# Two plain blocks in place of three in three channel mixers, with low parts of weights on GpSimd and a 32-byte shift of token-mixer tiles

## The chip, the cores and the metric

The kernel runs on one core of a Trainium2 chip. The metric is the device time of one execution in microseconds. The engines are TensorE (PE; PEld are its weight loads), VectorE (DVE), ScalarE (ACT), GpSimd (POOL) and SyncE (SP, which issues most DMAs). Each works through its own list of instructions in order and waits on semaphores for the others.

## The reference

A decoder trunk of two layers on 512 tokens of width 1024, in float32. Each layer has a channel mixer, a token mixer and another channel mixer:

```
for i in range(2):
    h = h + 0.5 * swiglu(rmsnorm(h, ffn_norm_a[i]), ffn_a_w_gate[i], ffn_a_w_up[i], ffn_a_w_down[i])
    m = rmsnorm(h, mix_norm[i])
    h = h + (mla_mixer, nsa_mixer)[i](m, ...)
    h = h + 0.5 * swiglu(rmsnorm(h, ffn_norm_b[i]), ffn_b_w_gate[i], ffn_b_w_up[i], ffn_b_w_down[i])
return rmsnorm(h, final_norm)

def swiglu(x, w_gate, w_up, w_down):
    return (silu(x @ w_gate) * (x @ w_up)) @ w_down      # 1024 -> 2816 -> 1024
```

## The kernel before

Everything stays in SBUF transposed: `h` is eight tiles h0 to h7 of 128 channels by 512 tokens. A float32 product is made of three matmuls in the faster float32r form: each operand is split into a high part, rounded by ScalarE's copy, and a low part, the rest; then high x high, high x low and low x high are summed in PSUM (`mm3`, and the same three in `plain1` and `product`).

A channel mixer (`ffn`, called four times with idx 0 to 3; "second mixer" is idx 1, "third" idx 2, "fourth" idx 3) runs over 22 hidden blocks f of 128. The first `PLAIN = 3` blocks are plain: `plain` takes a weight slab of 128x1024 for the gate and one for the up projection, and for each of the eight chunks of `h` and each half of the tokens issues three matmuls of 256 columns, 96 for the block. The other 19 blocks use a scheme of seven products of sums in place of eight (`wsums` makes the sums of weights, `product` issues 12 matmuls per product, 84 for the block: `px`, `pq` and `pg` are its PSUM tiles). For that scheme the input is needed as sums too. `combine(p)` makes them for p = 0 to 3 from `h[p]` and `h[p + 4]`: two scaled copies on ScalarE (`y`, L267), three VectorE subtractions (`u`, L271 to L273) and a split (`four`, L205 on ScalarE and L206 on VectorE). The combines are spread over the plain blocks; in idx 1 to 3 as (0), (1), (2, 3).

A plain slab is loaded by SyncE into `wr` (two buffers) and split into `w` (two buffers, `wtiles`): `split` inside `slab_ahead` does the high part on ScalarE (L176) and the low part on VectorE in one step of 1024 columns (L178). If `lo_pool` is set, GpSimd makes the low part in two steps of 512 columns (L182). This is used in the token mixers only. `wsums` splits its slabs and sums through `Kern.split` (L205 and L206), eight VectorE steps for a block's sums and low parts, five of 512 columns and three of 1024.

After a block's products come `gate` (L433 to L435: `tg` from the gate's PSUM and the row of norm factors, silu on ScalarE), `act` (L444 or L446, then a split into `ah` and `al`) and, from block 3 on, units of the down projection over the previous three blocks (`unit`: a slab `wdr` split into `wd`, 9 matmuls of 512 columns into `pd`, and an addition into `h`, L457).

The norm of the input is not applied ahead of the products but to their results. At the start of a channel mixer the sums of squares of the last chunks are still being made: `sumsq` squares on ScalarE (L285, into a scratch tile `sq` with one buffer) and adds on GpSimd (L289, `s2`). `late` squares the last two chunks and `norm_col` sums over partitions on TensorE (`pc`, L311) and finds the inverse root on VectorE in twelve tiny steps (`small`, L294 to L304). In idx 2 and 3 `late` stands between the gate and up halves of block 0, in idx 1 behind both. After block 1 `norm_bcast` spreads the factors (`pb`, L323, and `row`).

`plain` asks for its slabs in the order of use; for idx 2 the first slab is split at the end of the mixer ahead (`ahead`, tile `ra`). The order on each engine is set by a scheduler that interleaves the recorded instructions, and `issue_after` holds some of them back.

The token mixers keep the negated norm factors in a tile of four columns of their own: `colq` in `mla` (L892, read by the softmax at L869) and `ncol` in `nsa` (L976, read at L1197 and L1236). `vtc` is a scratch of 12 columns whose columns 0 to 3 `rsqrt_col` uses while it finds the factors and not after. Tiles of one pool lie one behind another in SBUF, at steps of 32 bytes, and pools opened later lie behind them; so the size of `colq` and `ncol` decides where later tiles of the token mixers begin.

Of the kernel before, what the change touches and what calls it, by code (L numbers as in the profile page):

```python
# [11 lines left out]
F32 = mybir.dt.float32  # L12
# [6 lines left out]
P = 128  # L19
# [4 lines left out]
NF = FF // P  # L24
# [21 lines left out]
LASTK = 4  # L46
HS = S // 2
KP = KC // 2
PLAIN = 3
PAD = 16  # L50
TILES = 24
XC = P + 2
NG = 3
# [8 lines left out]
class Kern:  # L62
# [278 lines left out]
    def wsums(self, idx, f):  # L341


        nc, fp, w_gu = self.nc, self.fp, self.a["w_gu"]
        if f == PLAIN:

            rg = fp.tile([P, 1024], F32, tag="fr", bufs=3, name="rg")
        else:
            rg = self.wp.tile([P, 1024], F32, tag="wr", bufs=2, name="wr")
        nc.sync.dma_start(rg, w_gu[idx, f, 0])  # L350
        ru = fp.tile([P, 1024], F32, tag="fr", bufs=3, name="ru")
        nc.sync.dma_start(ru, w_gu[idx, f, 1])
        s1 = fp.tile([P, S], F32, tag="s1", bufs=1, name="s1")
        g0, g1, u0, u1 = rg[:, :S], rg[:, S:], ru[:, :S], ru[:, S:]

        def split(src, pool, tag, bufs):
            n = src.shape[1]
            if pool is self.wp:
                hi, lo = self.wtiles("half")
            elif n == 1024:  # L360
                hi, lo = self.sum_tiles(n)
            else:
                hi = pool.tile([P, n], F32R, tag=tag[0], bufs=bufs, name="wh")
                lo = pool.tile([P, n + 2 * PAD], F32R, tag=tag[1], bufs=bufs, name="wl")[:, 2 * PAD :]
            with self.tc.issue_after(self.evicted.ins) if f == PLAIN + 1 else nullcontext():
                self.split(src, hi, lo)
            return [(hi[:, x : x + S].rearrange("p (k c) -> p k c", c=P), lo[:, x : x + S].rearrange("p (k c) -> p k c", c=P))
                    for x in range(0, n, S)]

        w = {}  # L370
        w[1], w[2] = split(rg, self.wp, None, 2)
        nc.vector.tensor_tensor(s1, u0, u1, op=ALU.add)
        nc.vector.tensor_tensor(u0, u0, g0, op=ALU.add)
        w[7], w[4] = split(ru, fp, ("fh", "fl"), 3)
        nc.vector.tensor_tensor(g0, g0, s1, op=ALU.add)
        nc.vector.tensor_tensor(g1, g1, g0, op=ALU.add)
        w[6], w[3] = split(rg, fp, ("fh", "fl"), 3)
        w[5], = split(s1, fp, ("sh", "sl"), 2)
        return w
# [44 lines left out]
    def ffn(self, idx, gain_next, ap, tp):  # L424
        nc, a = self.nc, self.a
        self.scr, self.fp = (tp, "sq", 1), tp
        ah, al, ht, row = {}, {}, [], None
        tg, tu, units = {}, {}, []

        def gate(f, g):  # L430
# [6 lines left out]
        def tu_tile():  # L437
            return self.xp.tile([P, S], F32, tag="w2", bufs=2, name="tu")

        def act(f):  # L440
            t = tu[f]
            if f < PLAIN:
                t = tu_tile()
                nc.vector.scalar_tensor_tensor(t, tu[f], -1.0, tg[f], op0=ALU.mult, op1=ALU.mult)  # L444
            else:
                nc.vector.tensor_tensor(t, t, tg[f], op=ALU.mult)  # L446
            ah[f] = ap.tile([P, S], F32R, tag="act", bufs=4 * NG, name="ah")
            al[f] = ap.tile([P, S], F32R, tag="act", bufs=4 * NG, name="al")
            self.split(t, ah[f], al[f])
# [34 lines left out]
            return self.norm_col(D, self.s2)  # L484


        gates = [self.bank("T", "pg") for _ in range(PLAIN)]
        for f, g in enumerate(gates):
            u = tu[f] = self.bank(("mm", "S")[f % 2], "pu")
            if idx == f == 0:  # L490
# [29 lines left out]
            elif f:  # L520
                gate(f, g)
                act(f)
            for p in (((0,), (1,), (2, 3)) if idx else ((0, 1), (2,), (3,)))[f]:
                self.combine(p)
        t = self.tiny
        for i, g in enumerate(gates[::-1]):
            nc.scalar.activation(t[:, i + 1 : i + 2], g[:, 0:1], AF.Identity, bias=t[:, i : i + 1])

        tail = PLAIN + (NF - 2 - PLAIN) // NG * NG
        for f in range(PLAIN, NF):  # L530
            if f % NG == 0 and f <= tail:
                units = [partial(unit, b0=f - NG, c=c) for c in range(KC)]
                left = NG if f < tail else NF - tail
            n = -(-len(units) // left)
# [24 lines left out]
        if gain_next == "fin":  # L559

            hs, out = [self.parts(self.four(F32)) for _ in range(4)], []
            for t in range(4):
                for b in range(2):
                    p = self.mm_bank("ph")
# [9 lines left out]
        for c in self.order:  # L574
            p = self.mm_bank("pd")
# [143 lines left out]
    def mla(self, gain_next):  # L719
        nc, tc, a = self.nc, self.tc, self.a  # L720
        with ExitStack() as cx:
            mp = cx.enter_context(tc.tile_pool(name="mla", bufs=1))
# [60 lines left out]
            p = self.proj(a["mla_w_in"][5], P, xh, xl, "pr")  # L783
# [49 lines left out]
            def query_slab(t):  # L833
                return self.slab_ahead(a["mla_w_q"][t], (3, P), "act")
# [3 lines left out]
            def rows_of(w):  # L838
                return self.proj(None, P, cqh, cql, "pq", w)
# [49 lines left out]
                self.w_o1(w, oh[:4], ol[:4], c2 + KP * e, e, False)  # L889

            pq = [rows_of(query_slab(t)()) for t in range(3)]
            colq = mp.tile([P, 4], F32, name="colq")  # L892
            nc.vector.tensor_scalar(colq, self.norm_col(QL, s2q), -MLA_SCALE, None, op0=ALU.mult)
            wv = self.slab_ahead(a["mla_w_v"][0], (2, S), raw=self.xp.tile([P, 2 * S], F32, tag="x", bufs=KC, name="vr"))
            wk = self.slab_ahead(a["mla_w_k"][0:2].rearrange("a p c -> p a c"), (2, 2, P))
# [72 lines left out]
    def nsa(self, gain_next):  # L968
        nc, tc, a = self.nc, self.tc, self.a
        with ExitStack() as cx:  # L970
            mp = cx.enter_context(tc.tile_pool(name="nsa", bufs=1))
# [1 line left out]
            rvalid = self.gains[:, 53:57]  # L973
            gat = mp.tile([P, 4, 3 * H], F32, name="gat")
            gcmp = mp.tile([P, 4, H], F32, name="gcmp")
            ncol = mp.tile([P, 4], F32, name="ncol")  # L976


            kc = mp.tile([P, 96 + 2 * G * P + 32], F32R, name="kc")
# [543 lines left out]
```

## Time and profile before

| | us |
|---|---|
| runs of the kernel, median (lowest to highest) | 1866.38 (1865.87 to 1868.28) |
| the profiled execution, its own time | 1868.31 |
| its span, first to last instruction | 1866.5 |
| second, third and fourth mixer's first matmul | 548.97, 886.40, 1518.82 |
| their first product block's first matmul | 583.37, 920.47, 1553.22 |
| their next block's first matmul, after the units | 599.37, 936.52, 1569.48 |

The mean granted TensorE clock is 0.999 of full speed. In the rows of the trace a matmul's own duration (278 ns for 256 columns, 391 ns for 512) is longer than the step from one to the next, since matmuls overlap; the steps from start to start are what add up.

### The profile page before, as it was taken

The page shows a single profiled execution, that of the slowest core. Times are in us where ns is not written, and L with a number is a line of the kernel's source. Part 1 is how long each engine was busy: PE and PEld are TensorE (multiplying, and loading weights), DVE is VectorE, ACT ScalarE, POOL GpSimd, SP SyncE. Part 2 cuts the span into 40 slices and gives each one's busy share as a digit, 9 for nine tenths or more (in the row PEclk, how much of TensorE's full clock was granted, in tenths as well). Part 3 has the DMA queues.
Part 4 walks back from the last instruction along what each step waited for, and adds up shares of the span by engine and source line. Part 5 has one row for each costly group of instructions (what it writes and reads, how often), then busy time and mean ns, then how long its engine had stood idle before and what let it go on. Part 6 is the DMA issues. An engine that isn't in the chain of part 4 may idle for free.

```text
span 1866.5 us, 32992 instructions
## 1 busy us (share of the span) xinstructions
PE 1851.3 (99%) x12448; PEld 1687.5 (90%) x12448; DVE 1506.4 (81%) x2810; ACT 1068.2 (57%) x1997; POOL 296.4 (16%) x370
## 2 busy tenths in 40 slices
PE   9999999999999999999999999999999999999998
PEld 8999999888889999998999999988888889999997
DVE  8988886688779888886898888666877888888885
ACT  7555553567666555554655455445776865555554
POOL 0000000258830000001000000022666620000000
PEclk9999999999999999999999999999999999999999
DMA  6333331334433333322433332162433133333321
GB/s 236 126 114 102 102 91 47 116 101 106 114 122 112 118 102 102 107 77 67 136 124 111 106 106 84 44 175 86 110 108 102 37 119 122 114 105 106 102 77 70
DMA packets 84336, 196.38 MB, mean 105 GB/s; under 512 B 10945, under 2 KB 38465, under 8 KB 84177
## 3 DMA queue, kind: packets, MB, share of 16 engines
q1 hardware_dynamic: 81664, 191.34, 33.6%
q10 hardware_dynamic: 2512, 2.93, 0.5%
q8 instruction: 98, 1.61, 0.4%
q14 instruction: 62, 0.50, 0.1%
HBM read 178.44 MB, written 2.16 MB: 97 GB/s over the span
## 4 chain that ended last, share of the span: by engine, by line
PE 89%; DVE 4%; ACT 1%; issue 1%; POOL 1%; DMA 1%; SPq 0%; ACTq 0%; DVEq 0%; POOLq 0%
PE pd L198 8%; PE pd L197 8%; PE pd L199 8%; PE px L388 5%; PE px L386 5%; PE px L387 5%; PE pg L386 4%; PE pg L388 4%; PE pg L387 4%; PE pq L388 3%; PE pq L387 3%; PE pq L386 3%; PE o L1326 2%; PE pt L1299 2%; PE po L197 1%; PE po L199 1%
## 5 line engine op out<-in xcount | busy, mean ns | idle before, releaser
L198 PE MATMUL pd<-al,wd 128*128 128x512 f32 x576 | 225.3, 391 | 0.0
L197 PE MATMUL pd<-ah,wd 128*128 128x512 f32 x576 | 225.1, 391 | 0.0
L199 PE MATMUL pd<-ah,wd 128*128 128x512 f32 x576 | 224.9, 390 | 0.0
L289 POOL TENSOR_TENSOR s<-s,sq 128x512 f32<-128x512 f32 x38 | 54.8, 1441 | 1052.8 <-ACT sq L285 1052.7
L206 DVE TENSOR_TENSOR w<-wr,w 128x1024 fp32r<-128x1024 f32 x72 | 88.2, 1225 | 134.8 <-ACT w L205 134.5
L386 PE MATMUL px<-four,wh 128*128 128x256 f32 x608 | 168.7, 278 | 0.4 <-ACT pg L543 0.3
L388 PE MATMUL px<-four,wl 128*128 128x256 f32 x608 | 168.4, 277 | 0.2 <-DVE wl L206 0.2
L386 PE MATMUL pq<-four,wh 128*128 128x256 f32 x608 | 168.2, 277 | 0.0
L387 PE MATMUL px<-four,wh 128*128 128x256 f32 x608 | 168.2, 277 | 0.0
L388 PE MATMUL pq<-four,wl 128*128 128x256 f32 x608 | 168.1, 277 | 0.0
L387 PE MATMUL pq<-four,wh 128*128 128x256 f32 x608 | 168.1, 276 | 0.0
L457 DVE SCALAR_TENSOR_TENSOR h<-pd,h 128x512 f32<-128x512 f32 x216 | 148.6, 688 | 13.6 <-PE pd L199 13.6
L205 ACT ACTIVATE wd<-wdr 128x384 fp32r<-128x384 f32 x192 | 99.2, 519 | 95.8 <-ACT wd L205 58.1
L176 ACT ACTIVATE w<-wr 128x1024 fp32r<-128x1024 f32 (+3 forms) x89 | 80.8, 908 | 84.1 <-PE pd L199 19.2
L199 PEld LDWEIGHTS pd<-ah,wd 128*128 128x128 f32 x576 | 108.3, 188 | 22.7
L197 PEld LDWEIGHTS pd<-ah,wd 128*128 128x128 f32 x576 | 108.2, 188 | 20.4
L198 PEld LDWEIGHTS pd<-al,wd 128*128 128x128 f32 x576 | 108.2, 188 | 19.3
L178 DVE TENSOR_TENSOR w<-wr,w 128x1024 fp32r<-128x1024 f32 (+3 forms) x75 | 78.4, 1046 | 49.4 <-ACT w L176 49.0
L717 ACT ACTIVATE p<-p,small 128x512 f32<-128x512 f32 (+2 forms) x192 | 106.9, 558 | 19.3 <-DVE small L716 15.4
L386 PEld LDWEIGHTS px<-four,wh 128*128 128x128 f32 x608 | 114.2, 188 | 1.7 <-ACT pg L543 0.8
L388 PEld LDWEIGHTS px<-four,wl 128*128 128x128 f32 x608 | 114.2, 188 | 0.8 <-DVE wl L206 0.6
L386 PEld LDWEIGHTS pq<-four,wh 128*128 128x128 f32 x608 | 114.2, 188 | 0.4 <-ACT uq L545 0.4
(379 smaller groups left out, 6163.5 us busy)
## 6 DMA issues: line engine op xcount, KB each, us to landing
wr<-in_w_gu SPq DMA_DIRECT2D x93, 512.0 KB, 3.3
ru<-in_w_gu SPq DMA_DIRECT2D x76, 512.0 KB, 4.1
wdr<-in_w_down SPq DMA_DIRECT2D x192, 192.0 KB, 2.4
wr<-in_w_down SPq DMA_DIRECT2D x24, 256.0 KB, 2.7
wr<-in_mla_w_o SPq DMA_DIRECT2D x8, 512.0 KB, 3.8
th<-btab_d SPq DMA_DIRECT2D x16, 256.0 KB, 3.7
wr<-in_nsa_w_q SPq DMA_DIRECT2D x8, 512.0 KB, 3.9
wr<-in_nsa_w_o SPq DMA_DIRECT2D x8, 512.0 KB, 3.8
```

The source lines that it names most:

```text
L176: self.copied = nc.scalar.activation(wh[:, m], raw[:, m], AF.Copy)
L178: nc.vector.tensor_tensor(wl[:, m], raw[:, m], f32v(wh[:, m]), op=ALU.subtract)
L197: mm(out, wh, xh, start=first, stop=False)
L198: mm(out, wh, xl, start=False, stop=False)
L199: return mm(out, wl, xh, start=False, stop=last)
L205: nc.scalar.activation(hi, src, AF.Copy)
L206: (nc.gpsimd if pool else nc.vector).tensor_tensor(lo, src, f32v(hi), op=ALU.subtract)
L386: mm(out, wh[:, p], xh, start=first and p == 0, stop=False, skip_group_check=True)
L387: mm(out, wh[:, p], xl, start=False, stop=False, skip_group_check=True)
L388: mm(out, wl[:, p], xh, start=False, stop=last and p == KP - 1, skip_group_check=True)
L457: nc.vector.scalar_tensor_tensor(self.h[c], p, 0.5, self.h[c], op0=ALU.mult, op1=ALU.add)
L717: nc.scalar.activation(p_sb[:, :n], p_sb[:, :n], AF.Exp, bias=nm, scale=-1.0, accum_out=sm)
```

## The change

The number of plain blocks becomes an attribute of the mixer: 3 for idx 0 and 2 for the others. In these, block 2 is a product block without units (its first units still come with block 3), the combines are made two at a time after blocks 0 and 1, and while the plain blocks are recorded `lo_pool` is set, so that the low parts of their slabs go to GpSimd. `colq` and `ncol` use columns 0 to 3 of `vtc` in place of tiles of their own, and the tiles behind them move down by 32 bytes.

```diff
-PLAIN = 3
...
 def wsums(self, idx, f):
-        if f == PLAIN:
+        if f == self.plains:
             rg = fp.tile([P, 1024], F32, tag="fr", bufs=3, name="rg")
...
-            with self.tc.issue_after(self.evicted.ins) if f == PLAIN + 1 else nullcontext():
+            with self.tc.issue_after(self.evicted.ins) if f == self.plains + 1 else nullcontext():
                 self.split(src, hi, lo)
...
 def ffn(self, idx, gain_next, ap, tp):
+        self.plains = 2 if idx else 3
+        self.lo_pool = idx > 0
...
-            if f < PLAIN:
+            if f < self.plains:
...
-        gates = [self.bank("T", "pg") for _ in range(PLAIN)]
+        gates = [self.bank("T", "pg") for _ in range(self.plains)]
...
-            for p in (((0,), (1,), (2, 3)) if idx else ((0, 1), (2,), (3,)))[f]:
+            for p in (((0, 1), (2, 3)) if idx else ((0, 1), (2,), (3,)))[f]:
                 self.combine(p)
+        self.lo_pool = False
...
-        tail = PLAIN + (NF - 2 - PLAIN) // NG * NG
-        for f in range(PLAIN, NF):
-            if f % NG == 0 and f <= tail:
+        tail, left = (NF - 2) // NG * NG, 1
+        for f in range(self.plains, NF):
+            if f % NG == 0 and NG <= f <= tail:
...
-            colq = mp.tile([P, 4], F32, name="colq")
+            colq = self.vtc[:, 0:4]
...
-            ncol = mp.tile([P, 4], F32, name="ncol")
+            ncol = self.vtc[:, 0:4]
```

GpSimd's list from the end of the first token mixer to the start of the second. `s` with a number is the sum of squares of one norm, `w` and `wr` a slab and its raw form, `p` and `ol` belong to the token mixer ahead. Before:

```order
L206 TENSOR_TENSOR ol<-o_6041,oh 128x512
L871 TENSOR_SCALAR p<-p,small 128x256
L871 TENSOR_SCALAR p<-p,small 128x128
L289 TENSOR_TENSOR s_6248<-s_6248,sq 128x512 x7
L289 TENSOR_TENSOR s_10107<-s_10107,sq 128x512 x7
L289 TENSOR_TENSOR s_13982<-s_13982,sq 128x512 x6
```

The same place in the changed kernel, where the lines 289 and 182 are 288 and 181:

```order
L288 TENSOR_TENSOR s_6247<-s_6247,sq 128x512 x4
L181 TENSOR_TENSOR w<-wr,w 128x512 x2
L288 TENSOR_TENSOR s_6247<-s_6247,sq 128x512
L181 TENSOR_TENSOR w<-wr,w 128x512 x2
L288 TENSOR_TENSOR s_6247<-s_6247,sq 128x512 x2
L181 TENSOR_TENSOR w<-wr,w 128x512 x4
L288 TENSOR_TENSOR s_10119<-s_10119,sq 128x512 x6
L181 TENSOR_TENSOR w<-wr,w 128x512 x2
L288 TENSOR_TENSOR s_10119<-s_10119,sq 128x512
L181 TENSOR_TENSOR w<-wr,w 128x512 x4
```

In the second mixer (the sum s_6247) eight pieces stand among the seven sums, for the four slabs of two plain blocks; in the third (s_10119) six, since its first slab is split in the mixer ahead; the seventh sum now stands behind the pieces of block 0's up slab.

VectorE's list in the third mixer, towards the end of the plain blocks (`four` is the last combine's low part, `wl<-ru` and `w<-rg` are low parts for the first product block, `tg`, `tu`, `al` belong to the plain blocks' gate and act). Before:

```order
L206 TENSOR_TENSOR wl<-ru,wh 128x1024
L206 TENSOR_TENSOR four<-u,four 128x1024
L178 TENSOR_TENSOR w<-wr,w 128x1024
L206 TENSOR_TENSOR wd<-wdr,wd 128x384 x2
L178 TENSOR_TENSOR w<-wr,w 128x1024
L433 TENSOR_TENSOR tg<-pg,row 128x512 x2
L435 TENSOR_TENSOR tg<-tg,row 128x512 x2
L444 SCALAR_TENSOR_TENSOR tu<-pu,tg 128x512 x2
L206 TENSOR_TENSOR al<-tu,ah 128x512
L433 TENSOR_TENSOR tg<-pg,row 128x512
L206 TENSOR_TENSOR w<-rg,w 128x1024
```

The same place in the changed kernel:

```order
L205 TENSOR_TENSOR four<-u,four 128x1024
L205 TENSOR_TENSOR wl<-ru,wh 128x1024
L205 TENSOR_TENSOR wd<-wdr,wd 128x384 x2
L205 TENSOR_TENSOR w<-rg,w 128x1024
L374 TENSOR_TENSOR rg<-rg,s_10612 128x512
L375 TENSOR_TENSOR rg<-rg 128x512
L371 TENSOR_TENSOR s_10740<-ru 128x512
L205 TENSOR_TENSOR wd<-wdr,wd 128x384
L372 TENSOR_TENSOR ru<-ru,wr 128x512
L205 TENSOR_TENSOR wl<-rg,wh 128x1024
L434 TENSOR_TENSOR tg<-pg,row 128x512 x2
```

The two slabs of the third plain block (L178) are gone, and the whole of the first product block's sums and low parts, down to `wl<-rg`, stands ahead of the plain blocks' gates, which came first before.

## The prediction

> **What bounds the kernel now.** First the page's engine totals, then busy time by stage.
>
> ```profile
> PE 1851.3 (99%) x12448; PEld 1687.5 (90%) x12448; DVE 1506.4 (81%) x2810; ACT 1068.2 (57%) x1997; POOL 296.4 (16%) x370
> ```
>
> TensorE has something to do for 1851.3 of 1866.5 us, so the time falls only where its instruction list gets shorter or each step quicker, and every wait that the change puts into that list is paid in full. The stages say how close the next engine is. In the next view a row is a stretch of time (us from the start), its length, then busy time of PE, PEld, DVE, ACT and POOL with instruction counts.
>
> ```profile
> core 0: us, PE busy (x) PEld busy (x) DVE busy (x) ACT busy (x) POOL busy (x), PEclk, DMA share, GB/s
> 886.40:920.47 34.07, 34.07 (x301) 34.07 (x300) 32.41 (x57) 23.68 (x36) 2.75 (x2) 1.00 0.50 169
> 898.24:903.68 5.44, 5.44 (x51) 5.44 (x49) 5.44 (x13) 2.71 (x4) 0.00 (x0) 1.00 0.29 95
> 909.47:920.47 11.00, 11.00 (x99) 11.00 (x98) 9.82 (x16) 5.97 (x11) 0.00 (x0) 1.00 0.41 133
> 936.52:946.09 9.57, 9.57 (x86) 9.57 (x85) 9.54 (x15) 5.56 (x10) 0.00 (x0) 1.00 0.42 141
> 200.00:300.00 100.00, 100.00 (x727) 93.86 (x726) 84.49 (x130) 53.11 (x86) 0.00 (x0) 1.00 0.29 87
> ```
>
> The first row is the three plain blocks of the third mixer: VectorE is busy for 32.41 of 34.07 us there, against 84.49 of 100 in steady product blocks. VectorE is therefore the near bound exactly where the change works. The second row is half a plain block (48 matmuls in 5.44 us, 0.113 us each), the third the whole block that goes (11.00 us), the fourth the 84 matmuls of a product block, without down-projection units (9.57 us). The clock is 1.00 in all of them.
>
> **The change part by part.** *The block.* Each of three mixers exchanges 11.00 us of TensorE for 9.57: 1.43 us saved, 4.3 in all.
>
> *GpSimd's low parts.* Two rows of GpSimd, then three of VectorE, from the start of the third mixer (start, length, engine, line, operation):
>
> ```profile
> 887.00 1.30 POOL L289 TENSOR_TENSOR s<-s,sq 128x512 f32<-128x512 f32 x1 [2.46 <-ACT sq L285]
> 889.08 1.45 POOL L289 TENSOR_TENSOR s<-s,sq 128x512 f32<-128x512 f32 x1 [0.79 <-ACT sq L285]
> ```
>
> ```profile
> 887.90 1.47 DVE L178 TENSOR_TENSOR w<-wr,w 128x1024 fp32r<-128x1024 f32 x1 [0.45 <-ACT w L176]
> 889.30 1.78 DVE L209 SCALAR_TENSOR_TENSOR x<-h,ngains,x 128x512 fp32r<-128x512 f32 x1
> 891.00 0.68 DVE L271 TENSOR_TENSOR u<-y 128x512 f32<-128x512 f32 x1
> ```
>
> They take turns. VectorE's subtraction at 887.90 could go on only when GpSimd ended at 888.30; GpSimd's second add, at 889.08, lasts 1.45 instead of 1.30; and L209, queued at 889.30, ends at 891.08, 0.55 us after GpSimd's 890.53. So while both read two SBUF tensors, a GpSimd instruction takes its whole length from VectorE. Its price is read from the same operation in the token mixer:
>
> ```profile
> 503.54 2.56 POOL L182 TENSOR_TENSOR w<-wr,w 128x512 fp32r<-128x512 f32 x2
> 506.08 1.26 POOL L871 TENSOR_SCALAR p<-p,small 128x512 f32<-128x512 f32 x2
> ```
>
> Two pieces take 2.54 us start to start, 1.27 each, where VectorE did a slab in 1.14 (from 905.08 to 906.22 below). Moving a slab's low part takes 1.14 from VectorE's list and puts 2.54 of turns in its way. The Trainium skill, "SBUF — State Buffer", section "Who interferes with whom", calls it an exclusive lock held for a whole instruction, against VectorE operations with two SBUF inputs and not those with one. By that exception only reads of PSUM could pass a piece, and beside the pieces the order has only the 4-column `small<-pc`; the sum would change by under 0.1 us.
>
> *VectorE's list in the third mixer.* Its steps, from starts of successive rows:
>
> ```profile
> 886.83 1.05 ACT L176 ACTIVATE w<-wr 128x1024 fp32r<-128x1024 f32 x1
> ```
>
> ```profile
> 902.67 0.16 DVE L304 SCALAR_TENSOR_TENSOR small<-small 128x4 f32<-128x4 f32 x1
> 902.74 0.42 DVE L272 TENSOR_TENSOR u<-y,u 128x256 f32<-128x256 f32 x1
> 903.08 0.69 DVE L373 TENSOR_TENSOR ru<-ru,rg 128x512 f32<-128x512 f32 x1
> 903.68 0.42 DVE L273 TENSOR_TENSOR u<-y,u 128x256 f32<-128x256 f32 x1
> 904.01 0.69 DVE L206 TENSOR_TENSOR wl<-s,wh 128x512 fp32r<-128x512 f32 x1
> 904.62 0.56 DVE L206 TENSOR_TENSOR wd<-wdr,wd 128x384 fp32r<-128x384 f32 x1
> 905.08 1.22 DVE L206 TENSOR_TENSOR wl<-ru,wh 128x1024 fp32r<-128x1024 f32 x1
> 906.22 1.23 DVE L206 TENSOR_TENSOR four<-u,four 128x1024 fp32r<-128x1024 f32 x1
> ```
>
> A 4-column step takes 0.07, 256 columns 0.33, 512 columns 0.60, 384 columns 0.46, 1024 columns 1.14. In the changed order, from the split of h7 (L209) to the low part `wl<-ru` that block 3's second product reads, VectorE has 20 steps of 512 columns, 10 of 1024, 10 of 256, 3 of 384 and 12 of 4: 12.0 + 11.4 + 3.3 + 1.4 + 0.8 = 28.9 us. GpSimd's turns in the stretch are the seventh sum of squares and six pieces (up slab of block 0, both slabs of block 1): 7 x 1.27 = 8.9. The first piece starts at 888.30, when the sixth sum ends (887.00 + 1.30; the high part is ready at 887.88). The list is through at 888.3 + 28.9 + 8.9 = 926.1.
>
> TensorE without waits would need that slab at: 909.47 (end of block 1 and the broadcast), + 9.57 for block 2, + 1.37 for a product of block 3, + 0.23 for two matmuls = 920.6. It comes 5.5 us late, and nothing covers it: the waits are spread over earlier steps (the sum of squares before `pc`, the low halves of block 1's slabs, `wl<-rg` in block 2), but TensorE's list is serial and each moves the rest. From there on VectorE has room again (9.54 busy, but 6.15 of units follow in a three-unit block).
>
> *The other two mixers.* Where their first piece can start, and their stretches of TensorE:
>
> ```profile
> 549.22 1.06 ACT L176 ACTIVATE w<-wr 128x1024 fp32r<-128x1024 f32 x1 [1.26 <-PE po L199]
> ...
> 1519.78 1.30 POOL L289 TENSOR_TENSOR s<-s,sq 128x512 f32<-128x512 f32 x1 [1.33 <-ACT sq L285]
> ```
>
> ```profile
> 566.25:571.98 5.73, 5.69 (x51) 5.53 (x49) 5.48 (x15) 3.42 (x4) 0.00 (x0) 1.00 0.57 182
> 571.98:572.36 0.38, 0.38 (x5) 0.38 (x5) 0.00 (x0) 0.38 (x2) 0.00 (x0) 1.00 0.00 0
> 1536.43:1541.87 5.44, 5.44 (x50) 5.44 (x49) 4.50 (x6) 2.96 (x3) 0.00 (x0) 1.00 0.46 140
> 1541.87:1542.22 0.35, 0.35 (x6) 0.35 (x5) 0.00 (x0) 0.10 (x1) 0.00 (x0) 1.00 0.69 105
> 586.09:587.76 1.67, 1.66 (x14) 1.47 (x13) 1.54 (x3) 0.38 (x1) 0.00 (x0) 1.00 0.25 57
> 921.83:924.92 3.09, 2.99 (x26) 2.79 (x25) 2.37 (x4) 1.27 (x3) 0.00 (x0) 1.00 0.07 16
> 1555.94:1557.85 1.91, 1.67 (x14) 1.48 (x13) 1.78 (x3) 0.38 (x1) 0.00 (x0) 1.00 0.26 75
> ```
>
> Their orders hold one more 512-column step (29.5 us). Second mixer: two sums and six pieces, 10.2; from 550.28, through at 590.0; needed at 566.25 + 5.44 + 0.38 + 9.57 + 1.37 + 0.23 = 583.2; 6.8 late. Fourth: 8.9; from 1521.08, through at 1559.5; needed at 1542.22 + 11.17 = 1553.4; 6.1 late. What TensorE already loses there now is not lost twice: 0.29 + 0.31 in the second (5.73 and 1.67 against 5.44 and 1.36), 0.37 in the third (3.09 against 2.72), 0.55 in the fourth (1.91 against 1.36). Net: 6.8 - 1.43 - 0.60 = **4.8**, 5.5 - 1.43 - 0.37 = **3.7**, 6.1 - 1.43 - 0.55 = **4.1**: 12.6 us slower.
>
> *The 32 bytes.* Dropping the two 4-column tiles puts the later token-mixer tiles 32 bytes lower. Matmuls on such a tile, and on one that already lies at an offset of 64 in 128 bytes:
>
> ```profile
> 540.11 0.40 PE L198 MATMUL po<-ol,w 128*128 128x512 f32 x1
> ...
> 548.74 0.39 PE L199 MATMUL po<-oh,w 128*128 128x512 f32 x1
> ```
>
> ```profile
> 930.37 0.39 PE L197 MATMUL pd<-ah,wd 128*128 128x512 f32 x1
> ...
> 936.28 0.40 PE L199 MATMUL pd<-ah,wd 128*128 128x512 f32 x1
> ```
>
> 37 steps in 8.63 us (233 ns) against 26 in 5.91 (227 ns). `oh`, `ol` and `ohl` go from an offset of 96 to 64, as `ah` has: 336 `po` matmuls at 6 ns are 2.0 us; the 128 wide `o` products (L1326) at most 0.8. I take 2.2. The ends are +0.5 slower (nothing shows a moved tile that gets slower) and 2.8 faster. The same page of the skill, section "Door 1: The DMA port swizzle", gives SBUF lines of 16 bytes; by that a shift of 32 changes nothing and the total would be 2.2 us more. The two rates speak against it, though on different tiles.
>
> **Sum:** -2.2 + 12.6 = +10.4. The profiled execution took 1868.3 us (span 1866.5), so 1878.7; it stands 1.9 above the median of the runs, 1866.4, from which it is **1876.8**.
>
> **The rivals.** *Faster.* The six pieces find gaps in VectorE's list. Without them VectorE would be through at 888.3 + 28.9 + 1.3 = 918.5, 2.1 us before 920.6, and TensorE would never wait: the change gives 4.3, the 1.5 of present waits and 2.2, that is 1858.4. The point that decides is 2.1 us for six pieces, 0.35 each. Against it: 32.41 busy of 34.07 leaves few gaps, and the turn-taking rows. For it: no row here shows L182 itself beside a VectorE step with two SBUF inputs.
>
> *No change.* Pieces cost half (0.63): 3.8 us less per mixer, so 1.0, -0.1 and 0.3 are left, less 2.2: 1865.4.
>
> *ScalarE as well.* The slabs' high parts (L176) stand behind the `four` splits in its list, and these wait for VectorE; if each mixer loses a further 1.5 us so, and the shift gives nothing, 1883.5. *The shift alone fails*, by the 16-byte rule or otherwise: 1879.0.
>
> **How the numbers follow.** Forecast with its two variants 0.62 (1871 to 1884), no change 0.16, faster 0.22 (1858 to 1862.6). About 0.2%, 3.7 us, is what a measurement of this kernel can tell from no change. The range goes from 1860.0 to 1883.0; outside remain the best end of the faster case and the worst of the slow one.
>
> **What would show it.** Right: in the third mixer VectorE steps of L271 to L273 and L206 stretched by 1.2 us beside GpSimd's L181; `pc` later than 891.89; TensorE waiting for POOL `w` in block 1 and for DVE `wl` in blocks 2 and 3; block 3's units ending some 4 us later than the 936.52 of now; `po` at 227 ns. Wrong: VectorE steps of ordinary length beside the pieces, or block 3 ending before 935.

## The result and the profile after

| | before | after |
|---|---|---|
| runs, median (lowest to highest), us | 1867.33 (1865.87 to 1869.71) | 1886.58 (1885.89 to 1888.07) |
| after / before | | 1.0102 (95% interval 1.0090 to 1.0114) |
| span of the profiled execution | 1866.5 | 1884.7 |

The change costs 19.2 us. It was forecast to cost 10.4, so the sign was right and the size too small. The totals of the page after, answering to the first line of the prediction:

```profile
PE 1855.2 (98%) x12412; PEld 1687.7 (90%) x12412; DVE 1529.3 (81%) x2823; ACT 1075.9 (57%) x2012; POOL 331.7 (18%) x392
```

TensorE has 36 matmuls fewer, 12 for each block exchanged, and yet takes longer. By stage, from first matmuls in both traces:

| stage, us | before | after | difference |
|---|---|---|---|
| start to the second mixer | 548.97 | 547.61 | -1.36 |
| second mixer, first matmul to the end of block 3's units | 50.40 | 57.24 | +6.84 |
| on to the third mixer | 287.03 | 286.67 | -0.36 |
| third mixer, the same stretch | 50.12 | 55.78 | +5.66 |
| on to the fourth | 582.30 | 582.16 | -0.14 |
| fourth mixer, the same stretch | 50.66 | 57.99 | +7.33 |
| the rest of the span | 297.02 | 297.25 | +0.23 |

Everything that is lost is lost in the three stretches that the prediction walked through. The third mixer after, by busy time in windows (columns as in the prediction): two plain blocks, block 2, block 3 with its units.

```profile
891.52:917.01 25.49, 23.96 (x206) 23.37 (x204) 24.18 (x38) 17.21 (x24) 12.50 (x8) 1.00 0.42 146
917.01:930.77 13.76, 10.22 (x87) 9.82 (x85) 12.64 (x19) 9.03 (x17) 0.00 (x0) 1.00 0.31 109
930.77:947.30 16.53, 16.39 (x114) 14.79 (x112) 16.36 (x26) 9.13 (x16) 0.00 (x0) 1.00 0.34 108
```

The two plain blocks took 23.07 before (886.40 to 909.47) and now 25.49, with GpSimd busy for 12.50; block 2 takes 13.76 in place of 9.57, with VectorE busy for 12.64 of it. GpSimd's pieces (L181) and, from the timeline of VectorE, what lies beside the second pair:

```profile
893.38 3.03 POOL L181 TENSOR_TENSOR w<-wr,w 128x512 fp32r<-128x512 f32 x2
896.37 1.72 POOL L288 TENSOR_TENSOR s<-s,sq 128x512 f32<-128x512 f32 x1
901.43 3.53 POOL L181 TENSOR_TENSOR w<-wr,w 128x512 fp32r<-128x512 f32 x2 [3.34 <-ACT w L175]
908.92 3.00 POOL L181 TENSOR_TENSOR w<-wr,w 128x512 fp32r<-128x512 f32 x2 [3.97 <-ACT w L175]
```

```profile
900.96 0.16 DVE L299 TENSOR_SCALAR small<-small 128x4 int32<-128x4 int32 x1
901.03 1.22 DVE L205 TENSOR_TENSOR four<-u,four 128x1024 fp32r<-128x1024 f32 x1
902.16 1.27 DVE L301 SCALAR_TENSOR_TENSOR small<-small 128x4 f32<-128x4 f32 x1
903.36 0.41 DVE L272 TENSOR_TENSOR u<-y,u 128x256 f32<-128x256 f32 x1
903.70 1.27 DVE L302 TENSOR_TENSOR small<-small 128x4 f32<-128x4 f32 x1
904.89 0.41 DVE L271 TENSOR_TENSOR u<-y,u 128x256 f32<-128x256 f32 x1
905.23 0.15 DVE L303 SCALAR_TENSOR_TENSOR small<-small 128x4 f32<-128x4 f32 x1
```

This is the turn-taking at its plainest. A step of four columns takes 0.15 us, but 1.27 when it has to let a piece pass (L301, L302); the pieces in turn stand behind VectorE's steps, 3.0 to 3.5 us for a pair whose work is 2.54. Between the two pieces of this pair VectorE gets L301 and the 256 columns of L272 through.

Where TensorE then waits (view of waits: us in total, times, longest), and the rows of ScalarE, VectorE and TensorE at the end of that wait:

```profile
PE px L385 <- ACT pg L545: 3.5, 1, 3.5
```

```profile
922.14 1.28 DVE L434 TENSOR_TENSOR tg<-pg,row 128x512 f32<-128x512 f32 x2
```

```profile
922.86 0.63 ACT L435 ACTIVATE tg<-tg 128x512 f32<-128x512 f32 x1 [1.53 <-DVE tg L434]
923.40 0.36 ACT L545 ACTIVATE pg<-px 128x256 f32<-128x256 f32 x1
```

```profile
923.81 0.39 PE L385 MATMUL px<-four,wh 128*128 128x256 f32 x1 [3.48 <-ACT pg L545]
```

The third product of block 2 needs the bank `px` back. The copy that frees it (L545) stands in ScalarE's list behind the silu of block 0's gate (L435), that waits for VectorE's multiplication (L434), and VectorE comes to it at 922.14, late by its list. In the first product block of before, the same copy (L543 there) stood behind no such wait, and the third product began 0.06 us after it:

```profile
923.04 0.36 ACT L543 ACTIVATE pg<-px 128x256 f32<-128x256 f32 x1
923.46 0.38 PE L386 MATMUL px<-four,wh 128*128 128x256 f32 x1
```

The prediction named VectorE's low parts (`wl`) as what TensorE would wait for in blocks 2 and 3; it is a copy on ScalarE, held up by VectorE's list at one remove. TensorE also waits for what GpSimd makes, as forecast: 2.5 us in all for `w` in block 1 of the three mixers and 2.5 for the sum of squares before `pc` in the third and fourth. The wait for the copy is 2.67 us in the second and 2.68 in the fourth mixer, and there the clock falls after it, which was not forecast at all (windows, the clock is the third figure from the right):

```profile
577.47:580.88 3.41, 1.04 (x8) 1.04 (x9) 3.41 (x6) 2.91 (x9) 0.00 (x0) 1.00 0.46 143
580.88:584.29 3.41, 3.41 (x18) 3.41 (x17) 3.29 (x7) 1.86 (x5) 0.00 (x0) 0.50 0.35 92
584.29:587.70 3.41, 3.41 (x31) 3.41 (x31) 2.38 (x4) 2.87 (x4) 0.00 (x0) 1.00 0.32 97
...
1557.10:1560.51 3.41, 1.39 (x13) 1.19 (x11) 3.38 (x6) 2.77 (x5) 0.00 (x0) 1.00 0.02 8
1560.51:1567.34 6.83, 6.17 (x29) 6.17 (x30) 5.37 (x10) 4.20 (x11) 0.00 (x0) 0.50 0.45 139
```

### The profile page after: what moved, and what is told of

It is laid out like the page before. It is cut to its first block, busy times and chain, and to the rows that moved or that the text cites. A ratio compares the mean times of both kernels' runs of the same rounds, so it can differ in the third digit from the quotient of the medians.

```text
span 1884.7 us, 32985 instructions
## 1 busy us (share of the span) xinstructions
PE 1855.2 (98%) x12412; PEld 1687.7 (90%) x12412; DVE 1529.3 (81%) x2823; ACT 1075.9 (57%) x2012; POOL 331.7 (18%) x392
## 4 chain that ended last, share of the span: by engine, by line
PE 87%; DVE 5%; ACT 2%; issue 1%; POOL 1%; DMA 1%; POOLq 0%; DVEq 0%; ACTq 0%
PE pd L197 8%; PE pd L198 8%; PE pd L196 8%; PE px L385 6%; PE px L386 6%; PE px L387 6%; PE pg L385 4%; PE pg L386 4%; PE pg L387 4%; PE pq L387 4%; PE pq L386 4%; PE pq L385 4%; PE o L1328 2%; PE pt L1301 2%; PE po L196 1%; PE po L198 1%
## 5 line engine op out<-in xcount | busy, mean ns | idle before, releaser
L385 PE MATMUL px<-four,wh 128*128 128x256 f32 x632 | 177.1, 280 | 9.0 <-ACT pg L545 8.8
L387 PE MATMUL px<-four,wl 128*128 128x256 f32 x632 | 175.6, 278 | 0.0
L386 PE MATMUL px<-four,wh 128*128 128x256 f32 x632 | 175.5, 278 | 0.0
L387 PE MATMUL pq<-four,wl 128*128 128x256 f32 x632 | 174.8, 277 | 0.0
L385 PE MATMUL pq<-four,wh 128*128 128x256 f32 x632 | 174.6, 276 | 0.0
L386 PE MATMUL pq<-four,wh 128*128 128x256 f32 x632 | 174.5, 276 | 0.0
L385 PEld LDWEIGHTS px<-four,wh 128*128 128x128 f32 x632 | 119.7, 189 | 12.0 <-ACT pg L545 9.8
L387 PEld LDWEIGHTS px<-four,wl 128*128 128x128 f32 x632 | 119.6, 189 | 0.5 <-DVE wl L205 0.2
L175 ACT ACTIVATE w<-wr 128x1024 fp32r<-128x1024 f32 (+3 forms) x83 | 74.5, 897 | 79.7 <-PE pd L198 19.2
L386 PEld LDWEIGHTS px<-four,wh 128*128 128x128 f32 x632 | 119.7, 189 | 0.0
L387 PEld LDWEIGHTS pq<-four,wl 128*128 128x128 f32 x632 | 118.7, 188 | 0.7 <-DVE wl L205 0.7
L385 PEld LDWEIGHTS pq<-four,wh 128*128 128x128 f32 x632 | 118.6, 188 | 0.4 <-ACT uq L547 0.4
```

What stands on the lines that cost most here:

```text
L175: self.copied = nc.scalar.activation(wh[:, m], raw[:, m], AF.Copy)
L385: mm(out, wh[:, p], xh, start=first and p == 0, stop=False, skip_group_check=True)
L386: mm(out, wh[:, p], xl, start=False, stop=False, skip_group_check=True)
L387: mm(out, wl[:, p], xh, start=False, stop=last and p == KP - 1, skip_group_check=True)
```

## The experiments

Two theories stood against each other. **Turns**: GpSimd's pieces take VectorE's time, so VectorE is late, and TensorE with it. **Room**: two plain blocks leave too little time for the gates and the first sums, whoever makes the low parts; or TensorE waits for GpSimd's results themselves. All times are medians; the ratio is to the kernel before, run on the same chip (1867.6 to 1868.3 in these runs).

### The parts one by one

**Low parts back on VectorE**, two plain blocks and the shift kept:

```diff
-        self.lo_pool = idx > 0
+        self.lo_pool = False
```

> The changed kernel with one part undone: VectorE makes the low parts of the plain blocks' slabs again, two plain blocks and the 32-byte shift stay. Turn theory (GpSimd's six pieces take VectorE's turns): each mixer gives back six turns of 1.27 us and takes three slabs of 1.14, so 4.2 us, and the two stretches at half clock (3.4 and 6.8 us long in the changed kernel's trace, 1.7 and 3.1 us lost) go with the waits that precede them: 1886.6 - 12.6 - 4.8 = about 1869, between 1866 and 1873. Room theory (two plain blocks leave too little time for the gates and the first sums, whoever makes the low parts; TensorE's long wait is for a copy that stands behind a silu on ScalarE): the wait of 2.7 to 3.5 us before the third product of block 2 stays in each mixer, and the time stays above 1878.

Measured: 1869.60, ratio 1.0007 (0.9998 to 1.0016); no half-clock stretch in its trace. The turn theory's number, 1869, is met, in part by luck: it holds 4.8 us for half-clock stretches, of which the runs that fill TensorE's waits, below, get nothing back. The room theory's 1878 is out. But this kernel is 1.8 us slower than the one before (from 0.4 faster to 3.0 slower), where the prediction's own steps make it 2.3 faster; so two plain blocks do not bring what was forecast even without pieces.

**Pieces alone**, three plain blocks:

```diff
         ah, al, ht, row = {}, {}, [], None
+        self.lo_pool = idx > 0
...
                 self.combine(p)
+        self.lo_pool = False
```

> The kernel before with one part of the change alone: GpSimd makes the low parts of the plain blocks' slabs in the second to fourth mixer (ten pieces a mixer), three plain blocks and the old addresses stay. Turn theory: ten turns of 1.27 us less five slabs of 1.14 put 7.0 us into VectorE's list of a mixer, which has 1.7 us of room in the plain blocks of the third mixer: 4 to 5 us a mixer and possibly some half-clock stretches, 1878 to 1886. Room theory: with the third plain block the gates still lie beside plain matmuls and the pieces find gaps: at most 1.5 us a mixer, 1867 to 1872.

Measured: 1883.42, ratio 1.0081 (1.0066 to 1.0096). GpSimd has 34 pieces more here than in the kernel before (12, 10 and 12 a mixer, since in the second and fourth the first slab is moved too). A plain block more does not hide them: 15.6 us for 34, 0.46 each, within the turn theory's range.

**The shift alone, and the change without it:**

```diff
-            colq = mp.tile([P, 4], F32, name="colq")
+            colq = self.vtc[:, 0:4]
...
-            ncol = mp.tile([P, 4], F32, name="ncol")
+            ncol = self.vtc[:, 0:4]
```

> The kernel before with the 32-byte shift alone. The prediction's rate theory (po matmuls 233 to 227 ns): 2.2 us faster, 1865.1. The traces' own balance (second mixer starts 1.36 us earlier after the change, the stretch from block 3 of the third mixer to the start of the fourth is 0.14 us shorter): 1.0 to 1.6 us faster, 1865.7 to 1866.3. Theory that addresses do not matter: 1867.3.

> The changed kernel without the 32-byte shift (the two small columns have tiles of their own again). If the shift works alone and by itself, as much slower than the changed kernel as the shift alone makes the kernel before faster: 1.0 to 2.2 us, 1887.6 to 1888.8. If it is the shift that lets waits or half-clock stretches arise in the mixers, below 1884.

Measured: alone 1867.32, ratio 0.9995 (0.9986 to 1.0005), 0.5 us faster with an interval from 2.6 faster to 0.9 slower; the change without it 1887.91, ratio 1.0106 (1.0091 to 1.0121), 0.9 slower than with it (20.1 us above its own kernel before, against 19.2). For a part of the matmuls the rate is as forecast. The 91 `po` matmuls ahead of the second mixer, before and with the shift alone (windows of that tile):

```profile
527.69:548.97 21.28, 21.28 (x91) 16.88 (x91) 4.83 (x7) 1.00 0.36 117
```

```profile
527.88:548.67 20.79, 20.79 (x91) 16.80 (x91) 4.82 (x7) 1.00 0.37 120
```

They start 0.2 us later and end 0.3 earlier: 5.4 ns a matmul. The 85 ahead of the fourth mixer do not gain, before and with the shift alone:

```profile
1498.87:1518.82 19.95, 19.95 (x85) 15.63 (x85) 4.70 (x7) 1.00 0.29 92
```

```profile
1498.33:1518.25 19.92, 19.92 (x85) 15.62 (x85) 4.69 (x7) 1.00 0.29 89
```

So the shift works for a part of the matmuls and is small.

### The price of a piece

**Fewer pieces**, those of block 0 only:

```diff
+            self.lo_pool = False
             for p in (((0, 1), (2, 3)) if idx else ((0, 1), (2,), (3,)))[f]:
```

> The changed kernel with GpSimd making the low parts of block 0's slabs only; those of block 1 go back to VectorE. Four fewer pieces in each of the three mixers (4, 2 and 2 are left of 8, 6 and 6). Turn theory, by the price of 2 turns of 1.27 us less 1.14 of VectorE, 1.4 us a slab: above the kernel with none (1869.6) by 1.4 for each slab that is left, four slabs, 5.6 us: 1875, between 1872 and 1878, more if a half-clock stretch comes with it. If only the pieces of block 1 cost (those of block 0 start while VectorE waits for h7): 1869 to 1871.

Measured: 1874.97, ratio 1.0040 (1.0025 to 1.0055). The trace has 10 pieces (4, 2 and 4), not 8, and the change 22 (8, 6 and 8). Above the kernel without pieces that is 5.6 us for 10, taking each against its own kernel before (7.4 - 1.8), and 17.5 for 22 (19.25 - 1.8): 0.56 a piece in block 0, and (17.5 - 5.6) / 12 = 0.99 in block 1. The prediction's price was 1.27 - 1.14 / 2 = 0.70.

**Turns or lateness of the results?** In the next two GpSimd makes nothing that anybody reads. VectorE makes the low parts; beside them GpSimd subtracts into a tile that is never read, or fills it.

```diff
+            if self.junk is not None:
+                for x in range(0, n, S):
+                    nc.gpsimd.tensor_tensor(self.junk.rearrange("p (a b) -> p a b", b=P), self.ident[:, None, :].to_broadcast([P, 4, P]), f32v(wh[:, x : x + S]).rearrange("p (a b) -> p a b", b=P), op=ALU.subtract)
```

> Two plain blocks with the low parts on VectorE (the run of 1869.6), and beside them GpSimd makes subtractions of the same size at the same places (20 of 128x512, 8, 6 and 6 a mixer, from a constant and the slab's high part into a tile that nobody reads): GpSimd's turns without anything that waits for GpSimd. Turn theory: 20 x 1.27 = 25 us more in VectorE's lists, nearly all of it late, and half-clock stretches on top: 1890 to 1901. Latency theory (the pieces cost because TensorE waits for low parts that GpSimd makes late): nobody waits for the dummies, 1869 to 1873.

```diff
+            if self.junk is not None:
+                nc.gpsimd.tensor_tensor(self.junk[:, 0:1], self.ident[:, 0:1], f32v(wh[:, 0:1]), op=ALU.subtract)
+                for x in range(0, n, S):
+                    nc.gpsimd.memset(self.junk, 0.0)
```

> As the run with dummy subtractions, but GpSimd fills the unread tile with zeros (20 fills of 128x512, each pair behind a subtraction of one column that starts it), so that it writes without reading a tile. By the turn theory as the Trainium skill words it (SBUF - State Buffer, Who interferes with whom: a VectorE instruction with two SBUF inputs contends with a GpSimd instruction that reads SBUF, not with one that only writes it) VectorE isn't held: 1869 to 1872. If any work of GpSimd takes VectorE's turns: as with the subtractions, by the length of a fill.

Measured: dummy subtractions 1892.18, ratio 1.0127 (1.0110 to 1.0144); fills 1870.74, ratio 1.0014 (1.0005 to 1.0023). Nobody waits for a dummy, and 22 of them (the expectation has 20) cost 22.2 us over the kernel without. So turns alone are enough for a loss of this size; a part of the 17.5 us, up to the 5 us of direct waits above, may still be lateness of GpSimd's results. A pair of fills of the second run, and VectorE beside it:

```profile
895.53 1.12 POOL L182 MEMSET junk<- 128x512 f32 x2
```

```profile
895.34 0.16 DVE L306 SCALAR_TENSOR_TENSOR small<-small 128x4 f32<-128x4 f32 x1
895.41 0.42 DVE L277 TENSOR_TENSOR u<-y,u 128x256 f32<-128x256 f32 x1
895.75 0.16 DVE L307 TENSOR_TENSOR small<-small 128x4 f32<-128x4 f32 x1
895.82 1.22 DVE L178 TENSOR_TENSOR w<-wr,w 128x1024 fp32r<-128x1024 f32 x1
```

All four steps have their ordinary length. A fill takes 0.53 us, so 22 that took turns would cost some 11 us; this kernel is 0.8 us above the one without. What the Trainium skill ("SBUF — State Buffer", section "Who interferes with whom") says of instructions that only write, quoted in the expectation, holds here: fills take no turns.

### Where the rest is: order, clock, VectorE's load

**Gates later**, in the kernel without pieces: the calls of `gate` and `act` for blocks 0 and 1 moved behind the fifth product of block 2.

```diff
             self.evicted = nc.scalar.activation(g[:, HS:], x, AF.Copy)
+            if idx and f == 2:
+                for e in range(2):
+                    gate(e, gates[e])
+                    act(e)
```

> Two plain blocks, low parts on VectorE, the shift (the run of 1869.6), and in the second to fourth mixer the gates and activations of blocks 0 and 1 (four splits, multiplications and silus, 4.8 us of VectorE) issued behind the fifth product of block 2 in place of ahead of its first. Theory that what is left there is the order (the copy of px stands behind the silu, the low part of rg behind the rest of the list): 1 to 2 us a mixer come back, 1863.5 to 1866.5, faster than the kernel before. Theory that VectorE's sum of work is the bound and not its order: the same waits come one block later, 1868 to 1872.

Measured: 1868.76, ratio 1.0007 (0.9998 to 1.0017). The scheduler put the gates where they had been: their first multiplication still follows the low part of `rg`, 26.7 us after the third mixer's first matmul in both kernels. So the run tells nothing of the order. The next one forces it.

**The copy ahead of the silus**, in the changed kernel with all pieces (the calls moved as above, and):

```diff
-            nc.scalar.activation(t, t, AF.Silu, scale=-1.0)
+            with self.tc.issue_after(self.freed.ins) if idx and f < 2 else nullcontext():
+                nc.scalar.activation(t, t, AF.Silu, scale=-1.0)
...
-            nc.scalar.activation(g[:, :HS], x, AF.Copy)
+            self.freed = nc.scalar.activation(g[:, :HS], x, AF.Copy)
```

> The changed kernel (GpSimd's pieces and all) with one order on ScalarE changed in the second to fourth mixer: the two silus of blocks 0 and 1 are issued behind the copy pg<-px of block 2, which stood behind the first of them and released TensorE after its waits of 2.7, 3.5 and 2.7 us. Queue theory (the copy's place is what costs): most of these 8.9 us come back, 1878 to 1881. List theory (VectorE is late with everything that follows, whatever releases TensorE first): the wait moves to a later step, the low part of rg or the products of block 3, and the time stays within 1884 to 1888.

Measured: 1883.25, ratio 1.0082 (1.0067 to 1.0097), between the two. TensorE's waits in its third mixer:

```profile
PE px L385 <- ACT uq L551: 1.3, 1, 1.3
PE px L385 <- ACT pg L547: 1.2, 1, 1.2
PE pc L310 <- POOL s L288: 1.0, 1, 1.0
PE pu L402 <- POOL w L181: 0.5, 1, 0.5
```

The 3.5 us fall apart into 1.2 and 1.3, the second again behind a copy on ScalarE, and the third mixer gains 0.3 us (55.78 to 55.51): VectorE is late with what follows, as the list theory has it. The gain is in the other two, 57.24 to 56.12 and 57.99 to 55.67. These are the two with half-clock stretches, and the profiled execution of this run has none.

**The same order without pieces** (VectorE makes the low parts):

> Two plain blocks, low parts on VectorE, the shift (the run of 1869.6), and the copy pg<-px ahead of the silus. In that run the copy stood ahead already in the third mixer, and the waits there are 0.3 to 0.6 us: 0 to 1 us come back, 1868.5 to 1869.6, by either theory; below 1867 the place of the copy costs more than its waits show.

Measured: 1869.79, ratio 1.0010 (1.0001 to 1.0019). No gain, as expected.

**Filling the wait.** In the changed kernel, first at the wait in block 2, then also at the wait for `pc` (`fill` issues its 14 matmuls into block 0's up bank):

```diff
-            self.product(7, w, q, True, False)
+            for _ in range(3 if idx and f == 2 else 1):
+                self.product(7, w, q, True, False)
```

> The changed kernel with the second product of block 2 (the pq one, 12 matmuls) issued three times in the second to fourth mixer; each time it starts the same sum anew, so nothing else changes. The 24 extra matmuls of 0.113 us, 2.7 us, lie where TensorE waits 2.7, 3.5 and 2.7 us for its third product. Theory that the half clock comes from TensorE's idle time: the two stretches of 3.4 and 6.8 us that follow those waits are gone, 1.7 and 3.1 us come back, and the extra matmuls cost at most 0.3 us a mixer: 1882 to 1883. Theory that the clock falls for another reason (the load, or chance): the stretches stay, 1886.6 or above. Theory that what is late is late by TensorE's own order: the extra matmuls move everything by 2.7 us, 1890 or above.

```diff
             if f == 0 and idx > 1:
+                self.fill(u, 14)
                 col = late()
```

> The changed kernel with both kinds of wait in the second to fourth mixer filled: the second product of block 2 issued three times as in the run before, and in the third and fourth mixer 14 extra matmuls of 0.113 us (1.6 us) into block 0's up bank, which its own first matmul clears, ahead of the four pc matmuls, where TensorE waits 1.0 and 1.6 us for the sum of squares. Idle theory (half the clock follows a cell of 3.41 us in which TensorE streamed little): all half-clock stretches are gone, none in any mixer, and the time falls to 1881 to 1884. Other theory: stretches stay, at other places or at these, and the time is 1886 or above.

Measured: 1886.50 and 1889.41, ratios 1.0099 (1.0084 to 1.0114) and 1.0113 (1.0098 to 1.0128). With the first fill the stretches behind block 2's wait are gone from the trace, and others have come behind the `pc` wait (3.41 us from 900.41, 6.8 from 1538.71); with both one is left (3.41 us from 1554.7). So the clock follows TensorE's idle time, but keeping it up bought nothing: the second kernel is the slowest of those in which GpSimd makes the low parts. That its fillers delay what stands behind them is likely, not shown. Both expectations of a gain missed.

**Relieving VectorE.** The low parts of the plain blocks from block 1 on are left out, in the kernel with two plain blocks and in the one with three:

```diff
-                if not self.lo_pool:
+                if not self.lo_pool and not self.skip_lo:
                     nc.vector.tensor_tensor(wl[:, m], raw[:, m], f32v(wh[:, m]), op=ALU.subtract)
...
+            if self.skip_lo:
+                wl = wh
```

> Two plain blocks, low parts on VectorE, the shift (the run of 1869.6), and the low parts of block 1's two slabs are left out in the second to fourth mixer: their matmuls take the high parts in their place, as many as before. VectorE loses two steps of 1.14 us a mixer, 2.3 us, 6.8 in all, TensorE's list stays. If VectorE's list is what holds the two-plain form (its exchange of 1.43 us of matmuls a mixer is there, but covered by lateness): 4.5 to 6.8 us come back, 1863 to 1865, faster than the kernel before. If the two-plain form costs for another reason (the order of block 3, in which the units stand between the products): 1868 to 1870.

> The kernel before (three plain blocks) with the low parts of the slabs of blocks 1 and 2 left out in the second to fourth mixer, the high parts taken in their place; VectorE loses four steps of 1.14 us a mixer, 13.7 us in all. If VectorE isn't late there: only the waits of 0.6, 0.4 and 0.6 us that its trace shows can come back, 1866 to 1868. If TensorE's pace there hangs on VectorE in a way that the waits don't show: below 1864.

Measured: 1868.22, ratio 0.9999 (0.9989 to 1.0008), and 1868.30, ratio 1.0001 (0.9991 to 1.0010). Three plain blocks do not hang on VectorE. With two, 6.8 us of VectorE's work bring only 1.8 us over the kernel that has it (1.8 slower than before, now 0.0), and not 4.5 or more. In the third mixer of the relieved kernel block 2 looks like this (block 2, then block 3, in windows):

```profile
909.08:920.33 11.25, 9.96 (x87) 9.76 (x86) 10.17 (x15) 8.89 (x17) 0.00 (x0) 1.00 0.19 64
920.33:936.88 16.55, 16.41 (x113) 14.74 (x112) 16.36 (x26) 9.16 (x16) 0.00 (x0) 1.00 0.33 108
```

VectorE has 1.1 us free in block 2 and TensorE still waits there, 1.29 us, for the copy behind the silu. In block 3 VectorE is busy for 16.36 of 16.55 us, although work was saved ahead of it. The gates cannot start before the norm's row is spread, after block 1. With a third plain block they lie beside its 96 matmuls; with two they fall into blocks 2 and 3, together with the sums of the next products.

**The same with the copy ahead of the silus:**

> The two-plain kernel without block 1's low parts (the run of 1868.2: high parts in their place) with the same order on ScalarE, the copy pg<-px ahead of the silus. In the run of 1868.2 TensorE waits 1.3 us there in the third mixer and 0.5 in the second. If the copy's place is what is left of the loss: 1 to 3 us come back, 1865 to 1867. If it is block 3, where VectorE makes the gates of blocks 0 to 2 and block 3's and 4's sums at once: 1868.

Measured: 1867.61, ratio 0.9996 (0.9986 to 1.0006). That is 0.7 us faster than the kernel before and 0.6 than the run of 1868.2, each less than a measurement can tell. Block 3 with its units, in the second, third and fourth mixer of this kernel:

```profile
580.96:598.31 17.35, 16.75 (x114) 14.68 (x112) 17.32 (x26) 9.79 (x17) 0.00 (x0) 1.00 0.30 103
919.01:935.59 16.58, 16.39 (x113) 14.77 (x112) 16.37 (x26) 9.20 (x16) 0.00 (x0) 1.00 0.33 108
1550.58:1567.49 16.91, 16.74 (x113) 14.68 (x112) 16.88 (x26) 9.33 (x15) 0.00 (x0) 1.00 0.31 106
```

By the prediction's figures TensorE needs 9.57 + 6.15 = 15.72 for such a block, so 3.7 us are lost here (1.2 before, where the same stretches took 16.00, 16.05 and 16.26), and VectorE is busy nearly throughout. Block 2 takes 9.91, 10.92 and 9.64 in place of 9.57, another 1.8. The 2.5 and the 1.8 are the 4.3 that the shorter matmul list saves. That VectorE's work is the cause in block 3 is read from these rows; no run takes work out of that block. No kernel run here beats the one before by more than a measurement can tell.

## Why the prediction fell short

- **Block swap, -1.43 a mixer: right as a count** (36 matmuls fewer), but it isn't seen in the time, because of the next point.
- **The list of two plain blocks without pieces: the first step that failed.** By the prediction's sums it would be late by 2.5, 1.3 and 1.9 us in the second, third and fourth mixer, which the swap and the present waits pay for: net -0.1 over the three. Measured is +1.8 without pieces, against -0.5 with the shift alone: +2.3, so 2.4 us were missing (from the scatter of the two runs, some 0.7 more or less). What failed is the sentence that VectorE has room again from block 3 on. Before, the first product block with its units had room for VectorE, 12.57 us busy of 16.05 (first row). In the kernel without pieces (third mixer: plain blocks, block 2, block 3, the other rows) block 3 has none:

```profile
920.47:936.52 16.05, 15.95 (x114) 14.68 (x113) 12.57 (x19) 9.57 (x15) 0.00 (x0) 1.00 0.19 66
```

```profile
886.16:909.24 23.08, 23.08 (x205) 23.07 (x204) 22.60 (x42) 17.52 (x25) 2.74 (x2) 1.00 0.54 186
909.24:920.02 10.78, 10.51 (x87) 9.98 (x86) 10.51 (x18) 8.22 (x16) 0.00 (x0) 1.00 0.28 85
920.02:936.96 16.94, 16.63 (x113) 14.88 (x112) 16.91 (x25) 9.41 (x16) 0.00 (x0) 1.00 0.31 105
```

  Block 2 takes 10.78 instead of 9.57, the forecast lateness; block 3 takes 16.94, where 9.57 + 6.15 = 15.72 were expected, with VectorE busy for 16.91. Over the three mixers block 3 is 3.1 us longer than that (16.76, 16.94 and 16.54), on top of some 5 us up to its start, near the 5.7 forecast. The prediction stopped its walk at block 3's second product.
- **GpSimd's turns: the mechanism is shown, the term was too small.** It stood for 12.6 us (18 x 1.27 for six pieces a mixer, less 9 x 1.14 for three slabs); the pieces cost 17.5. The kernel has 22: two ahead of the second and two ahead of the fourth mixer's first matmul were not counted, and at the prediction's 0.70 apiece 22 make 15.4; no run prices these four. And some 4 of the 17.5 (3.3 between the medians, 4.3 taking each against its own kernel before) come back when the copy `pg<-px` is put ahead of the silus, which neither the sum nor the rival with ScalarE had: that rival looked at L176 behind the `four` splits, and the one that mattered was L545 behind a silu. The prediction's walk itself held: VectorE's `wl<-ru` of block 3's second product was to be through 39.7 us after the third mixer's first matmul (926.1 - 886.4) and was after 40.8 (931.10 + 1.21 - 891.52), with 1.4 us of idle time that the walk did not have. Its remark that only reads of PSUM could pass a piece was too narrow, since two of the steps of four columns (L298 and L299 of the changed kernel) read a single SBUF tensor; at 0.07 us each nothing hangs on it.
- **The 32 bytes: right in the rate, too large in the sum.** Forecast -2.2; the two runs give -0.5 and -0.9. The 91 matmuls ahead of the second mixer gain 0.5 us; the 85 ahead of the fourth gain nothing that shows, and why is open. That the others, in groups of 12, gain little because they lie between waits of the token mixer is likely, not shown.
- Together: 2.4 + 4.9 (17.5 - 12.6) + 1.7 (shift alone) = 9.0, the difference between 10.4 and 19.2 us but for rounding. The three steps lead from the kernel before to the changed one, so they must add up; what the runs show is how the sum divides.
- **The rivals.** The faster case needed six pieces to cost 2.1 us; they cost several times that. The case of half the price fell with it. Most of the forecast's own checks came out as named: steps stretched by 1.1 us, `pc` late (898.14 is 6.62 us after the mixer's start, 5.49 before), TensorE waiting for GpSimd's `w` in block 1, block 3's units ending late (55.78 against 50.12). Waits for VectorE's low parts in blocks 2 and 3 came to 0.2 us at most; the copy on ScalarE stood in their place.
- **Open:** what half the clock costs. The two mixers that lost their stretches in the run with the copy ahead gained 1.1 and 2.3 us, the one without gained 0.3. But executions of that same kernel with a mean clock of 0.996 took 1883.06 and 1882.14, and those with 1.000 and 0.999 took 1883.43 and 1885.33. A stretch beside a late VectorE may cost nothing. So the 4 us above are not divided into queue and clock. Open is also which step of VectorE's list would have to leave block 3 for two plain blocks to pay.

## What to carry to other kernels

An engine that shares turns with the busiest one is no free engine: each piece of 1.27 us on GpSimd cost 0.6 to 1.0 us net (0.5 with three plain blocks), and a VectorE step of four columns waited 1.1 us for it. Where a block is exchanged for one with less matmul time but more side work, follow the near-bound engine to the point at which it is idle again, not to the first operand that is late. Look also at what stands behind a waiting instruction in a third engine's list: a copy that frees a bank belongs ahead of work that waits. Here that was worth 3.3 us with the pieces, and nothing without them.

## What the runs showed of the hardware

Half the clock comes in cells. In seven traces 16 such stretches were seen away from the ends of the span, of 3.41 or 6.8 us; within a trace their starts lie whole multiples of 3.413 us apart (in the changed kernel 580.88 and 1560.51, 287 cells). Counted from the matmuls' starts (0.113 us for 256 columns), TensorE had streamed for at most 0.37 of the cell ahead in 15 of the 16 (0.43 in one), while full-clock cells with 0.40 (from 918.80 in the changed kernel) and 0.43 (from 570.24 in the run with block 0's pieces only) were followed by none. So in these traces it isn't the length of a wait that decides but how it falls into the cells: the 3.48 us of the third mixer straddled two and left the clock alone, the 2.67 us of the second lay in one, but for 0.3. The Trainium skill, "TensorE: Matmul & The Clock Gate", section "What's actually happening", gives a free-running window of 3413 ns, and the distances here agree; its advice in the section "HAM oscillation — how this bites in real kernels", no idle gap over about 3.4 us, is not strict enough here, where 2.67 us were enough.
